# An encoder layer with a Strassen-like MLP: thirteen subtractions move from VectorE to GpSimd, and one weight split is issued later

## The chip, the cores and the metric

The kernel runs as one program on one core of a Trainium2 chip. The metric is the device time of one execution in microseconds (us). TensorE (PE) does the matmuls; a separate row, PEld, shows its weight loads. VectorE (DVE), ScalarE (ACT) and GpSimd (POOL) work on tiles, and SyncE (SP) as well as ACT issue DMA transfers. Every engine works through its own list of instructions in order.

## The reference, cut to what matters

```python
hn = rmsnorm(h, norm_mix); proj = hn @ w_in           # 1024 tokens, 1024 -> 2304
o_a = window_gqa_sink(...); o_b = neighbourhood_attention(...)
h = h + concat(rmsnorm(o_a), rmsnorm(o_b)) @ w_out
hn = rmsnorm(h, norm_ffn)
g, u = hn @ w_gate, hn @ w_up                         # 1024 -> 2816 each
g = depthwise_conv_width3(g) + conv_b
h = h + (silu(g) * u) @ w_down                        # 2816 -> 1024
return rmsnorm(h, norm_final)
```

All data are float32. The kernel keeps that precision on TensorE by splitting each factor into a rounded high part and the rest (the low part) and adding three products: high x high, low x high, high x low.

## The kernel before, in words

**Attention stage, to about 370 us.** The combined projection is cut into 18 tiles of 128 columns (class `Project`, L554). Each tile has weights for eight blocks of the input; they come in two loads of four blocks (`fetch_w`, L152), and each load is split by one ACT instruction that rounds it to the high part and one DVE instruction that subtracts (`halve_w`, L158; the records are L162 and L163). `load` splits the first half, `load_rest` (L562) the second. The generator `rest` (L744) runs through the jobs 3 to 17 and then the output projection, and hands its matmuls out as filler between the attention's own; inside job i, at its block number `REST` = 11 (L757), it calls `load_rest` of job i + 1. Job index 14 is tile 17, the last projected one; its `load_rest` holds its two instructions behind an attention split (`behind`, the second argument of `halve_w`). The order on PE is as written; on the other engines a scheduler sets the order when the program is built.

**MLP stage, from about 400 us.** gate and up are computed for 22 column tiles f, each with seven half-size products instead of eight (a Strassen-Winograd scheme on 2 x 2 halves of input and weights). The input's halves are kept in eight tiles `h1[k]`, `at(k, h)` being half h (512 columns) of tile k. From the normed input come four sums in place, each for k = 0 to 3 (`K1`): the first (`t1`, L1181) and second (`t2`, L1191) of `at(k, 1)`, then in one loop (L1197 to L1199) the third (`t3`, into `at(k, 0)`) and the fourth (`t4`, into `at(k, 1)`). Each sum is split by `operand` (L963): an ACT rounding (L966) and a DVE subtraction (L967), into tiles named `hg`.

A column tile is a `Gated` object (L1090). Its products are PE groups of twelve matmuls: p1 and p2 into the PSUM bank `x`, p5 and then p3 into `y`, p6, then p7 and p4 into `z`. The later group of a bank adds to what is there, and DVE reads the bank between the two (c<-y at L1110 between p5 and p3, gs<-z at L1117 between p6 and p7, c<-z at L1134 between p7 and p4). So p3 can't start on PE before L1110 is done. `conv` (L1123) is two ACT and two DVE instructions of twice the size. p4 ends with a product on DVE (L1140) and, for the first of a pair of column tiles, with a subtraction on the finished block (L1144); `keep` (L1153) sends blocks to DRAM by DMAs from ACT's queue. `sums` (L1159) makes three more subtractions for each pair of column tiles (L1163, L1164, L1167). All these subtractions go through the helper `sub` (L998), so all have the line L998 in the trace.

The first four column tiles, `units` (L1170), are computed together product by product: p5 of all four, p6, p3, p7, p4. Their weights are made by `head_weights` (L1002): loads into three buffers `raw`, a sum or difference on DVE, and the split (`split_w`, L943; ACT L948, DVE L949). After them a loop (L1290 on) takes one column tile at a time in the order p1, p5, p4 of the one before, p6, p2, p3, p7, with `w_next` making the next weights. `owed` (L1289) holds units 1 and 3, whose `sums` come in the first two turns.

GpSimd works in the attention stage: it scales the probabilities (L411), copies sinks (L402) and makes eight bias tiles (L481, L482). Later it has six multiplications at the very end (L1384). Between them it is idle.

Of the kernel before, what the change touches and what calls it, by code (L numbers as in the profile page):

```python
# [16 lines left out]
ALU = mybir.AluOpType  # L17
PSUM = bass.MemoryType.PSUM

D, S, HD = 1024, 1024, 64  # L20
KT = D // 128
NB = S // 128
HALF = 512
# [16 lines left out]
REST = 11  # L40
# [13 lines left out]
def hybrid_layer(tc, xT, w_first, w_in, w_out, w_gate, w_up, w_down, small, sink, rpb, consts, rope, out):  # L54
    nc = tc.nc
    with ExitStack() as ctx:
# [13 lines left out]
        def big(name, tag, dt=F32):  # L70
            return lpool.tile([128, S], dt, name=name, tag=tag, bufs=slots[tag])
# [25 lines left out]
        for name, dst, n in (("h", his, 2), ("h", his, 2), ("l", los, 2), ("l", los, 2), ("w", None, 2)):  # L97
            t = flat(big(name, "mix", F32R)[:, :], n)
# [46 lines left out]
        def behind(*names):  # L145

            stack = ExitStack()
            for n in names:
                stack.enter_context(tc.issue_after(mark[n].ins))
            return stack  # L150
# [7 lines left out]
        def halve_w(raw, held=False):  # L158

            hi, lo = (wpool.tile([128, 4, 128], F32R, name=n, tag=n) for n in ("whi", "wlo"))  # L160
            with behind(*["high", "rest"] * held):
                mark["weights"] = nc.scalar.activation(hi, raw, AF.Copy)  # L162
                mark["weights low"] = nc.vector.tensor_tensor(lo, raw, f32(hi[:, :, :]), op=ALU.subtract)  # L163
            return [(hi[:, j, :], lo[:, j, :]) for j in range(4)]
# [389 lines left out]
        class Project:  # L554
# [5 lines left out]
                self.w = halve_w(raw)  # L560

            def load_rest(self):  # L562
                self.w += halve_w(self.raw, self.m == 17)

            def run(self):
                self.t = tmp("t")
# [50 lines left out]
        xg, first = [None] * KT, [Project(m) for m in range(3)]  # L617
        third = first[2]
        jobs = [Project(m) for m in range(3, 18)] + [OutA(d) for d in range(KT)]

        def split_x(k, part=slice(0, S)):

            g, src = col(C_NMIX + k), xts[k][:, part]
            hi, lo = (t[:, part] for t in xg[k])
            pin(nc.scalar.activation(hi, src, AF.Copy, scale=g))
            pin(nc.vector.scalar_tensor_tensor(lo, src, g, f32(hi), op0=ALU.mult, op1=ALU.subtract))  # L626
# [48 lines left out]
        t = quarters(big("f", "mix"))  # L675
# [5 lines left out]
        for part in range(3):  # L681
            for p, ps in zip(first, banks):
                w, x = p.w[0], xg[0]
# [38 lines left out]
        def make_stacks(job):  # L722
            with tc.high_priority(offset=400):
                stacks(job.m, job.t)
            done.add(job.m)

        def settle(age):

            for item in list(later):
                item[0] -= 1  # L730
                if item[0] <= 0:
                    later.remove(item)
                    item[1]()
            while waiting and (len(waiting) > 1 or age >= (LATE if waiting[0].m == 3 else SOON if waiting[0].m == 17 else LAG)):
                m = waiting[0].m
                if live["op"] + needs(m) > slots["op"]:
                    break
                live["op"] += needs(m)
                with behind(*["stack", "low"] * (m == 3)):
                    waiting.pop(0).post()  # L740
# [3 lines left out]
        def rest():  # L744
            for i, job in enumerate(jobs):
                if i + 1 < len(jobs):
                    with behind(*[["spread", "root"], ["stack"]][i] if i < 2 else []):
                        jobs[i + 1].load()
                for n, _ in enumerate(job.run()):
                    yield True  # L750
                    if i == 0:
                        if n == 8:
                            with behind("copied"):
                                for p in first[:2]:
                                    make_stacks(p)
                        continue
                    if n == REST and i + 1 < len(jobs):  # L757
                        jobs[i + 1].load_rest()
                    settle(n)
                    if (i, n) in aux:  # L760
                        aux[i, n]()
                if i == 0:
                    with behind("stack", "copied"):
                        jobs[1].load_rest()
                    with behind("weights", "weights low"):
                        make_stacks(third)
                if isinstance(job, Project):
                    waiting.append(job)
                while len(waiting) > 2:
                    settle(0)  # L770
                    if len(waiting) > 2:
                        yield False
# [29 lines left out]
        for i in range(8):  # L802
            aux[13, 1 + i + i // 2] = normed_a(*divmod(i, 2))
        filler = rest()
        live["op"] = sum(needs(m) for m in range(3))

# [5 lines left out]
        units = []  # L812
        for g in range(2):
            for b in range(NB):
                q, t = unit_window(g, b)
# [53 lines left out]
        for u in range(len(flat)):  # L869
            q, t, need, kind = flat[u]  # L870
# [51 lines left out]
        for h in range(2):  # L922
            wide = widen(vb2[h], "pt")
            for i in range(4):
                x = mix[4 + i][:, tsl(h)]
# [31 lines left out]
        def group(ps, ws, xs, first, last):  # L957
            for i, (w, x) in enumerate(zip(ws, xs, strict=True)):
                nc.tensor.matmul(ps, w[0], x[0], start=first and i == 0, stop=False, skip_group_check=True)  # L959
                nc.tensor.matmul(ps, w[0], x[1], start=False, stop=False, skip_group_check=True)  # L960
                nc.tensor.matmul(ps, w[1], x[0], start=False, stop=last and i == len(ws) - 1, skip_group_check=True)  # L961
# [12 lines left out]
        at = lambda k, h: h1[k][:, tsl(h)]  # L974
# [20 lines left out]
        HEAD = 4  # L995
        FH = FT // 2
        FO = [f for k in range(FH) for f in (k, k + FH)]
        sub = lambda o, x, y: nc.vector.tensor_tensor(o, x, y, op=ALU.subtract)  # L998

        wsum = [fpool.tile([128, 4, 128], F32, name="ws", tag="tt", bufs=6) for _ in range(HEAD)]  # L1000

# [88 lines left out]
        class Gated:  # L1090
# [45 lines left out]
            def p4(self):  # L1136
                group(self.z, W[self.f, "22"], B["t4"], False, True)
                u = self.c
                nc.vector.tensor_tensor(u[:, 0:HALF], self.z, u[:, 0:HALF], op=ALU.add)
                nc.vector.tensor_tensor(u, u, self.cv, op=ALU.mult)  # L1140
                k = self.f % FH
                if self.f < FH:
                    first_of[k] = u
                    sub(u[:, HALF:S], u[:, HALF:S], u[:, 0:HALF])  # L1144
                    keep(u, ("11", k), ("t1", k))
                else:
                    keep(u, ("21", k), ("22", k))
# [5 lines left out]
        def keep(t, *names):  # L1153
            d = dram.tile([128, HALF * len(names)], F32, name="x", tag="x" + "_".join(f"{n}{k}" for n, k in names))
            nc.scalar.dma_start(d, t)
            for i, name in enumerate(names):
                X[name] = d[:, i * HALF:(i + 1) * HALF]

        def sums(unit):  # L1159
            k = unit.f % FH  # L1160
            a, b = first_of.pop(k), unit.c
            t = big("t23", "mix")
            sub(t[:, 0:HALF], b[:, HALF:S], a[:, HALF:S])  # L1163
            sub(t[:, HALF:S], t[:, 0:HALF], a[:, 0:HALF])  # L1164
            keep(t, ("t2", k), ("t3", k))
            t4 = half("t4")
            sub(t4, b[:, 0:HALF], t[:, 0:HALF])  # L1167
            keep(t4, ("t4", k))

        units = [Gated(f, ("o", "o", "pj", "pj")[i], ("s", "s", "pt", "pt")[i]) for i, f in enumerate(FO[:HEAD])]  # L1170
# [24 lines left out]
            head_weights(i, "s2")  # L1195
        B[2, 2] = [operand(at(k, 1), "op") for k in K2]
        for k in K1:  # L1197
            sub(at(k, 0), at(k, 1), at(k, 0))
            sub(at(k, 1), at(k + 4, 0), at(k, 1))  # L1199
        for i, u in enumerate(units):  # L1200
            u.p6()
            head_weights(i, "s4")
# [87 lines left out]
        for i, f in enumerate(FO[HEAD:]):  # L1290
            u = Gated(f)
# [8 lines left out]
            if pend:  # L1300
                pend.p4()
                if pend.f >= FH:
                    sums(pend)
# [4 lines left out]
            if owed:  # L1308
                sums(owed.pop(0))
# [24 lines left out]
            pend = u  # L1334
        pend.p4()
        sums(pend)


# [76 lines left out]
        for i, (p, j, c) in enumerate(order):  # L1415
# [4 lines left out]
            f, n = PARTS[c]  # L1420
# [146 lines left out]
```

## Time and profile before

| what | value |
|---|---|
| median of 3 runs | 1075.73 us (1075.58 to 1076.07) |
| the profiled execution's own time | 1076.77 us |
| its span, first to last instruction | 1075.0 us |
| granted TensorE clock | 0.997 |
| PE busy | 1063.8 us, 99% of the span, 5094 matmuls |
| DVE busy | 867.3 us, 81% |
| ACT busy | 555.7 us, 52% |
| POOL busy | 106.8 us, 10% |

What lies around the span is 1.77 us. Times inside the trace are microseconds from the start of the span. A row of the timeline has the start, the duration, the engine, the line, the operation, its output and input tiles with shapes, a count, and in brackets the time for which the engine stood idle before it and what ended that. Instructions of one engine overlap a little: the next one's start is often 0.1 us before the recorded end of the one before, so the distance between two starts, not the duration, is what an instruction takes of a full queue.

### The profile page before, as it was taken

The numbers are of one execution on the slowest core, as the hardware profiler recorded it, in microseconds if no ns is written. First come the engines' busy times: TensorE is split into PE (matmuls) and PEld (weight loads), VectorE is DVE, ScalarE is ACT, GpSimd is POOL, SyncE is SP. The second block draws the span as 40 slices with busy tenths as digits, with TensorE's granted clock in tenths as the row PEclk, the third lists the DMA queues.
The fourth block names the chain that finished last, engine by engine and source line by source line (L and its number), as shares of the span: only waits on it lengthen the run. The fifth ranks groups of instructions, "written<-read, shape, count | busy, mean of one in ns | idle before, by whom it ended". The sixth has DMA issues, their size and how long they took to land.

```text
span 1075.0 us, 14902 instructions
## 1 busy us (share of the span) xinstructions
PE 1063.8 (99%) x5094; PEld 889.6 (83%) x5094; DVE 867.3 (81%) x1596; ACT 555.7 (52%) x1059; POOL 106.8 (10%) x188
## 2 busy tenths in 40 slices
PE   9999999999999999999999999999999999999997
PEld 7888888888888888887788888888888888888887
DVE  7889887768878799899988877887887858897765
ACT  8457776647676554534434343432434645544451
POOL 1124333222332000000000000000000000000002
PEclk9999999999999999999999999999999999999998
DMA  7223122322234245214342232322222788867644
GB/s 278 74 74 80 40 69 60 89 69 79 78 88 148 96 156 210 78 56 162 135 157 98 106 110 81 129 106 108 98 89 101 251 288 308 270 216 241 222 139 157
DMA packets 68220, 144.94 MB, mean 135 GB/s; under 512 B 8240, under 2 KB 18736, under 8 KB 68144
## 3 DMA queue, kind: packets, MB, share of 16 engines
q1 hardware_dynamic: 57920, 118.69, 34.9%
q10 hardware_dynamic: 10224, 25.30, 6.2%
q8 instruction: 40, 0.66, 0.2%
q14 instruction: 36, 0.29, 0.1%
HBM read 103.58 MB, written 28.57 MB: 123 GB/s over the span
## 4 chain that ended last, share of the span: by engine, by line
PE 89%; DVE 7%; ACT 1%; issue 1%; DMA 1%; POOL 0%; SPq 0%; DVEq 0%; ACTq 0%
PE pj L170 8%; PE pj L172 8%; PE pj L171 8%; PE dn L959 7%; PE dn L961 7%; PE dn L960 7%; PE z L961 5%; PE z L959 5%; PE z L960 5%; PE s L381 3%; PE x L959 3%; PE x L961 3%; PE x L960 3%; PE y L961 3%; PE y L959 3%; PE y L960 3%
## 5 line engine op out<-in xcount | busy, mean ns | idle before, releaser
L948 ACT ACTIVATE whi<-ws 128x512 fp32r<-128x512 f32 (+1 forms) x100 | 60.3, 623 | 126.8 <-DVE ws L1066 82.5
L959 PE MATMUL dn<-xd,whi 128*128 128x512 f32 (+1 forms) x330 | 124.0, 376 | 0.0
L961 PE MATMUL dn<-xd,wlo 128*128 128x512 f32 (+1 forms) x330 | 123.7, 375 | 0.0
L960 PE MATMUL dn<-xd,whi 128*128 128x512 f32 (+1 forms) x330 | 123.7, 375 | 0.0
L961 PE MATMUL z<-hg,wlo 128*128 128x512 f32 x264 | 103.1, 390 | 0.9 <-DVE wlo L949 0.7
L170 PE MATMUL pj<-xgh,whi 128*128 128x512 f32 x245 | 103.3, 422 | 0.0
L959 PE MATMUL z<-hg,whi 128*128 128x512 f32 x264 | 103.0, 390 | 0.0
L960 PE MATMUL z<-hg,whi 128*128 128x512 f32 x264 | 102.8, 389 | 0.0
L407 ACT ACTIVATE p<-p,nm 128x385 f32<-128x385 f32 (+3 forms) x128 | 75.2, 587 | 50.8 <-DVE nm L403 49.7
L411 POOL TENSOR_SCALAR p<-p,sm 128x384 f32<-128x384 f32 (+1 forms) x128 | 78.1, 622 | 207.2 <-DVE sm L409 171.7
L171 PE MATMUL pj<-xgl,whi 128*128 128x512 f32 x245 | 96.2, 393 | 0.3 <-DVE xgl L626 0.3
L172 PE MATMUL pj<-xgh,wlo 128*128 128x512 f32 x245 | 96.4, 393 | 0.0
L949 DVE TENSOR_TENSOR wlo<-raw,whi 128x512 fp32r<-128x512 f32 (+1 forms) x102 | 66.4, 671 | 26.6 <-ACT whi L948 25.6
L418 DVE TENSOR_TENSOR pl<-pt,ph 128x384 fp32r<-128x384 f32 (+2 forms) x108 | 63.5, 589 | 24.9 <-ACT ph L417 23.5
L948 ACT ACTIVATE whi<-raw 128x512 fp32r<-128x512 f32 (+1 forms) x102 | 60.5, 612 | 44.6 <-DMA raw<-in_w_down_dram 19.8
L949 DVE TENSOR_TENSOR wlo<-ws,whi 128x512 fp32r<-128x512 f32 (+1 forms) x100 | 67.0, 683 | 19.1 <-ACT whi L948 17.9
L1384 POOL TENSOR_TENSOR h<-h,wide 128x256 f32<-128x256 f32 (+1 forms) x6 | 5.4, 918 | 707.4 <-ACT wide L1380 707.4
L417 ACT ACTIVATE ph<-pt 128x384 fp32r<-128x384 f32 (+2 forms) x108 | 55.2, 512 | 32.4 <-PE pt L517 24.7
L961 PEld LDWEIGHTS dn<-xd,wlo 128*128 128x128 f32 x330 | 62.1, 188 | 11.2
L960 PEld LDWEIGHTS dn<-xd,whi 128*128 128x128 f32 x330 | 62.1, 188 | 11.2
L959 PEld LDWEIGHTS dn<-xd,whi 128*128 128x128 f32 x330 | 62.1, 188 | 10.9
L1274 ACT ACTIVATE xd<-xd 128x512 fp32r<-128x512 f32 x77 | 47.6, 626 | 43.8 <-DMA xd<-x 42.1
(270 smaller groups left out, 2678.0 us busy)
## 6 DMA issues: line engine op xcount, KB each, us to landing
xd<-x SPq DMA_DIRECT2D x77, 256.0 KB, 4.8
raw<-in_w_down_dram SPq DMA_DIRECT2D x72, 256.0 KB, 3.8
raw<-in_w_gate_dram SPq DMA_DIRECT2D x22, 512.0 KB, 3.5
raw<-in_w_up_dram SPq DMA_DIRECT2D x22, 512.0 KB, 3.9
x<-c ACTq DMA_DIRECT2D x22, 512.0 KB, 3.3
raw<-in_w_in_dram SPq DMA_DIRECT2D x30, 256.0 KB, 2.8
raw<-in_w_down_dram SPq DMA_DIRECT2D x36, 192.0 KB, 4.2
x<-t ACTq DMA_DIRECT2D x11, 512.0 KB, 2.7
```

What stands on the lines that cost most here:

```text
L170: nc.tensor.matmul(ps, w[0], x[0][:, tsl(h)], start=first, stop=False)
L171: nc.tensor.matmul(ps, w[0], x[1][:, tsl(h)], start=False, stop=False)
L172: nc.tensor.matmul(ps, w[1], x[0][:, tsl(h)], start=False, stop=last)
L407: nc.scalar.activation(p[:, j, 0:e], p[:, j, 0:e], AF.Exp, bias=nm, scale=-1.0, accum_out=sm[:, j:j + 1])
L411: nc.gpsimd.tensor_scalar(p[:, i, 0:m], p[:, i, 0:m], sm[:, i:i + 1], 1.0, op0=ALU.mult, op1=ALU.mult)
L417: mark["high"] = nc.scalar.activation(ph[:, 0:n], ps[:, 0:n], AF.Copy)
L418: mark["rest"] = nc.vector.tensor_tensor(pl[:, 0:n], ps[:, 0:n], f32(ph[:, 0:n]), op=ALU.subtract)
L948: nc.scalar.activation(hi, src, AF.Copy)
L949: nc.vector.tensor_tensor(lo, src, f32(hi[:, :, :]), op=ALU.subtract)
L959: nc.tensor.matmul(ps, w[0], x[0], start=first and i == 0, stop=False, skip_group_check=True)
L960: nc.tensor.matmul(ps, w[0], x[1], start=False, stop=False, skip_group_check=True)
L961: nc.tensor.matmul(ps, w[1], x[0], start=False, stop=last and i == len(ws) - 1, skip_group_check=True)
```

## The change

The helper `sub` gets an argument for the engine. GpSimd then does

- the eight subtractions of the loop over `K1` that make the third and fourth sums;
- the subtraction at the end of p4 for column tiles among the first four (of which two, unit 0 and unit 2, are first of a pair);
- the three subtractions of `sums` for unit 1.

That is 8 + 2 + 3 = 13 subtractions of 128x512. And `load_rest` of the last projected tile is called in its own job, after its third block (n == 2), instead of at block 11 of the job before, and without being held behind the attention's split.

```diff
             def load_rest(self):
-                self.w += halve_w(self.raw, self.m == 17)
+                self.w += halve_w(self.raw)
...
         jobs = [Project(m) for m in range(3, 18)] + [OutA(d) for d in range(KT)]
+        last_in = jobs[14]
...
-                    if n == REST and i + 1 < len(jobs):
+                    if n == REST and i + 1 < len(jobs) and jobs[i + 1] is not last_in:
                         jobs[i + 1].load_rest()
+                    if n == 2 and job is last_in:
+                        job.load_rest()
...
-        sub = lambda o, x, y: nc.vector.tensor_tensor(o, x, y, op=ALU.subtract)
+        sub = lambda o, x, y, engine=nc.vector: engine.tensor_tensor(o, x, y, op=ALU.subtract)
...
                 if self.f < FH:
                     first_of[k] = u
-                    sub(u[:, HALF:S], u[:, HALF:S], u[:, 0:HALF])
+                    sub(u[:, HALF:S], u[:, HALF:S], u[:, 0:HALF], nc.gpsimd if self.f in FO[:HEAD] else nc.vector)
...
             t = big("t23", "mix")
-            sub(t[:, 0:HALF], b[:, HALF:S], a[:, HALF:S])
-            sub(t[:, HALF:S], t[:, 0:HALF], a[:, 0:HALF])
+            engine = nc.gpsimd if unit is units[1] else nc.vector
+            sub(t[:, 0:HALF], b[:, HALF:S], a[:, HALF:S], engine)
+            sub(t[:, HALF:S], t[:, 0:HALF], a[:, 0:HALF], engine)
             keep(t, ("t2", k), ("t3", k))
             t4 = half("t4")
-            sub(t4, b[:, 0:HALF], t[:, 0:HALF])
+            sub(t4, b[:, 0:HALF], t[:, 0:HALF], engine)
...
         for k in K1:
-            sub(at(k, 0), at(k, 1), at(k, 0))
-            sub(at(k, 1), at(k + 4, 0), at(k, 1))
+            sub(at(k, 0), at(k, 1), at(k, 0), nc.gpsimd)
+            sub(at(k, 1), at(k + 4, 0), at(k, 1), nc.gpsimd)
```

## The prediction

> **What bounds the kernel now.** I read the page's busy table first, then the busy time by stretches, then who PE waited for, and last the timeline around each wait.
>
> ```profile
> PE 1063.8 (99%) x5094; PEld 889.6 (83%) x5094; DVE 867.3 (81%) x1596; ACT 555.7 (52%) x1059; POOL 106.8 (10%) x188
> ...
> 460.00:490.00 30.00, 29.89 (x132) 24.48 (x131) 30.00 (x47) 13.46 (x19) 0.00 (x0) 1.00 0.21 70
> 490.00:520.00 30.00, 29.08 (x124) 22.57 (x124) 28.27 (x40) 13.27 (x19) 0.00 (x0) 1.00 0.44 160
> 600.00:700.00 100.00, 100.00 (x442) 82.79 (x442) 80.21 (x113) 41.03 (x61) 0.00 (x0) 1.00 0.30 105
> ```
>
> PE works 99% of the span, so what stops PE anywhere is added at the end, and nothing else counts. The columns of the stretches are length, PE, PEld, DVE, ACT, POOL, clock, DMA share, GB/s. In 600 to 700 PE is full and DVE has a fifth of its time to spare. In 460 to 490 DVE is full (30.00 of 30), in 490 to 520 nearly: there PE hangs on DVE. The PE timeline shows by how little:
>
> ```profile
> 488.99 0.39 PE L960 MATMUL z<-hg,whi 128*128 128x512 f32 x1
> 489.48 0.50 PE L961 MATMUL z<-hg,wlo 128*128 128x512 f32 x1
> ...
> 495.05 0.40 PE L960 MATMUL z<-hg,whi 128*128 128x512 f32 x1
> 495.78 0.50 PE L961 MATMUL z<-hg,wlo 128*128 128x512 f32 x1 [0.34 <-DVE wlo L949]
> ...
> 512.01 0.39 PE L960 MATMUL y<-hg,whi 128*128 128x512 f32 x1
> 512.58 0.50 PE L961 MATMUL y<-hg,wlo 128*128 128x512 f32 x1 [0.18 <-DVE wlo L949]
> ...
> 515.37 0.40 PE L960 MATMUL z<-hg,whi 128*128 128x512 f32 x1
> 516.17 0.50 PE L961 MATMUL z<-hg,wlo 128*128 128x512 f32 x1 [0.40 <-DVE wlo L949]
> ...
> 521.30 0.39 PE L959 MATMUL y<-hg,whi 128*128 128x512 f32 x1
> 521.52 0.39 PE L960 MATMUL y<-hg,whi 128*128 128x512 f32 x1
> ...
> 529.68 0.39 PE L960 MATMUL y<-hg,whi 128*128 128x512 f32 x1
> 530.36 0.49 PE L961 MATMUL y<-hg,wlo 128*128 128x512 f32 x1 [0.29 <-DVE wlo L949]
> ```
>
> Undisturbed, matmuls start 0.22 to 0.23 us apart (521.30 to 521.52). The five steps to a low weight part take 0.49, 0.73, 0.57, 0.80 and 0.68, together 2.1 us too much, and about 2.6 us with slow restarts of some 0.1 us each. That is all that a faster DVE could give back here.
>
> **What is removed.** DVE loses 13 subtractions.
>
> ```profile
> 453.24 0.74 DVE L989 SCALAR_TENSOR_TENSOR h<-h,par,sw 128x512 f32<-128x512 f32 x1
> 453.90 1.28 DVE L998 TENSOR_TENSOR h<-h,h 128x512 f32<-128x512 f32 x2
> ...
> 493.24 0.69 DVE L998 TENSOR_TENSOR ws<-raw 128x512 f32<-128x512 f32 x1 [0.20 <-DMA raw<-in_w_up_dram]
> ...
> 497.44 1.38 DVE L949 TENSOR_TENSOR wlo<-raw,whi 128x512 fp32r<-128x512 f32 x2 [0.51 <-ACT whi L948]
> ...
> 499.78 0.69 DVE L949 TENSOR_TENSOR wlo<-raw,whi 128x512 fp32r<-128x512 f32 x1 [0.36 <-ACT whi L948]
> ...
> 501.11 0.69 DVE L1139 TENSOR_TENSOR c<-z,c 128x512 f32<-128x512 f32 x1 [0.63 <-PE z L961]
> ...
> 517.84 0.68 DVE L1110 TENSOR_TENSOR c<-y,c 128x512 f32<-128x512 f32 x1
> 518.43 1.22 DVE L1140 TENSOR_TENSOR c<-c,cv 128x1024 f32<-128x1024 f32 x1
> ...
> raw<-in_w_gate_dram SPq DMA_DIRECT2D x22, 512.0 KB, 3.5
> ```
>
> An instruction of this size takes 0.60 us of a full queue (517.84 to 518.43). The mark by which I measure is the evacuation at 517.84, c<-y of the fifth column tile: p3 (PE, 521.30 in the fence above) adds to the same bank and can't start before it. Before, DVE is there 3.5 us early.
>
> The order of the built program's instructions shows what now stands ahead of that evacuation. Gone are ten subtractions (eight sums, two finished blocks): -10 x 0.60 = -6.0. New ahead of it are four weight splits and the product of unit 3 that stood behind: 4 x 0.60 + 1.2 = +3.6. DVE's idle time on the way was 0.20 + 0.51 + 0.36 + 0.63 = 1.7; with DVE earlier, the loads, which wait for buffers that DVE frees, show up more. I walked the new order with the old durations and 3.1 to 3.5 us for a weight load (3.5 is the table's median for the larger ones): my estimate is 3.8 us idle, +2.1. So without any other effect the mark starts at 517.84 - 6.0 + 3.6 + 2.1 = 517.5, and all five stalls would go.
>
> **What is added.** GpSimd gets 13 subtractions of 128x512, eight of them from about 454.6 us on, as soon as the first of the second sums (453.90) is there, and five from the first finished block on. Its price for such an operation, and what happens when it meets DVE:
>
> ```profile
> L1384 POOL TENSOR_TENSOR h<-h,wide 128x512 f32<-128x512 f32 x2 | 2.6, 1296 | 691.9 <-ACT wide L1380 691.9
> ...
> L481 POOL TENSOR_TENSOR xb<-cst,rr x8: 983/993/2987, 24.0 to 314.9; 128x384 f32<-128x384 f32 x8
> L482 POOL TENSOR_TENSOR xb<-cst,rr x8: 718/730/1707, 26.9 to 315.9; 128x256 f32<-128x256 f32 x8
> ...
> L163 DVE TENSOR_TENSOR wlo<-raw,whi x38: 670/685/1499, 29.6 to 368.9; 128x512 fp32r<-128x512 f32 x38
> ...
> 248.17 0.99 POOL L481 TENSOR_TENSOR xb<-cst,rr 128x384 f32<-128x384 f32 x1 [1.18 <-DVE nm L403]
> 249.12 1.17 POOL L482 TENSOR_TENSOR xb<-cst,rr 128x256 f32<-128x256 f32 x1
> ...
> 248.22 1.50 DVE L163 TENSOR_TENSOR wlo<-raw,whi 128x512 fp32r<-128x512 f32 x1
> 249.63 1.21 DVE L299 SCALAR_TENSOR_TENSOR kb<-t,cst,ka 128x512 fp32r<-128x512 f32 x1
> ...
> 308.31 1.41 DVE L299 SCALAR_TENSOR_TENSOR kb<-t,cst,ka 128x512 fp32r<-128x512 f32 x2
> ...
> 1050.07 2.55 POOL L1384 TENSOR_TENSOR h<-h,wide 128x512 f32<-128x512 f32 x2 [691.90 <-ACT wide L1380]
> ...
> 1050.02 4.04 DVE L1386 SCALAR_TENSOR_TENSOR h<-h,par,sw 128x512 f32<-128x512 f32 x6 [0.38 <-ACT wide L1380]
> ```
>
> At 248 us four instructions meet that each read two tiles from SBUF. L163 has a median of 0.69 and takes 1.50: it began 0.05 after L481 and lost 0.81. L482 has 0.73 and takes 1.17: it lost 0.44 to L163. L299, 0.70 at 308.31, takes 1.21: it lost 0.51 to L482. So the two engines exclude each other and take turns, though DVE's next instruction was always ready. A turn ends about 0.15 us before the recorded end (248.22 + 0.81 = 249.03 against 249.16). For GpSimd's 1.30 us that is 1.15 us in which DVE stands still. At 1050 DVE reads one tile from PSUM: L1386 runs at 4.04 / 6 = 0.67 beside a busy POOL, L989 at 453.24 to 453.90 takes 0.66 without it. So evacuations from PSUM run beside GpSimd.
>
> [...]
>
> DVE's queue from 454 on is full of weight and operand splits, which read two tiles from SBUF, so every GpSimd subtraction finds it busy. 13 x 1.15 = 14.9; three of them I expect beside an evacuation (0.60 each), -1.8: **+13.1 us** on DVE for 13 x 0.60 = 7.8 taken off. The mark starts at 517.5 + 13.1 = 530.6 and ends its read about 0.55 later: p3 starts at 531.1 instead of 521.30, **+9.8**. This includes all that PE loses on the way (behind the second sums' last block, at the third difference of weights) since DVE's queue alone leads to the mark. Behind it p7 waits for gs<-z two places on, which p3's twelve matmuls (2.7 us) cover. The stall at 529.68 goes, as DVE's remaining work is then no longer behind PE: -0.5.
>
> Also queued behind the new waits: on ACT, the split of the second sums' fourth block stands behind a split that waits for GpSimd's fourth subtraction, and the copy of the fifth tile's p1, which p2 needs, stands behind a DMA issue that waits for a GpSimd block. Both are over before the mark is, so they cost nothing extra. SP's queue is as before but for one pair of transfers swapped. GpSimd's later work (1050) is far off.
>
> **The later split.** It takes one ACT and one DVE instruction out of a crowded place:
>
> ```profile
> 301.51 0.69 DVE L163 TENSOR_TENSOR wlo<-raw,whi 128x512 fp32r<-128x512 f32 x1
> ...
> 304.14 0.38 PE L517 MATMUL pt<-cst,p 128*128 128x128 f32 x2
> 304.59 0.44 PE L528 MATMUL o<-ph,v 128*128 128x384 f32 x1
> 305.18 0.44 PE L529 MATMUL o<-pl,v 128*128 128x384 f32 x1
> ```
>
> From L528 to L529 PE takes 0.59 where a larger matmul takes 0.23, and two transposes and the wait for ph before take 0.45 (304.14 to 304.59). Without the split, the exponentials, and then ph and pl, come up to its 0.60 us earlier: between 0 and -0.6; I take the step's excess, -0.4. The split now stands at its job's third block. Its weights are first used by the ninth: six blocks of three matmuls, at least 6 x 3 x 0.23 = 4.1 us, cover it. Its transfer is issued as before, in `load`. Should the cover fail, it costs at most its own 0.6.
>
> **Sum:** +9.8 - 0.5 - 0.4 = +8.9 us on the profiled 1076.77, whose span is 1075.0 with 1.77 around it (1085.7). The profiled run is 1.04 above the median of the three, so on the median 1075.73 + 8.9 = **1084.6**.
>
> **Rivals.** *No exclusion in this stretch* (the mark 517.5): the stalls go, -2.6 - 0.4, 1072.7. For it speaks that GpSimd was idle there; against it the rows at 248. This one ends on the other side: it decides if a meeting costs DVE under about 0.25 us (p3 has 521.3 - 517.5 - 0.55 = 3.3 us to spare, over 13). *DVE wins when its queue is full* and GpSimd only slips in at evacuations: L481 once took 2.99 us, two more than its median, as if it lost several turns. Then a meeting costs 1.15 - 0.60: 7.2, p3 at 525.2, +3.9 - 0.5 - 0.4 = +3.0, 1078.7. *Losses and gains cancel* within the 0.2% (2.15 us, about what a measurement of this kernel tells from no change): meetings of about 0.3 us, 1075.7. That the change isn't made can't be: the built program has the 13 on POOL.
>
> **Chances.** The forecast (1080 to 1088) 0.60, DVE wins 0.12, cancel 0.11, no exclusion 0.17. So slower 0.72, same 0.11, faster 0.17. The range leaves out the faster case and the tails: 1074.5 to 1088.
>
> **What would show it.** Right: L998 on POOL from 454.6 on with 1.3 to 1.9 us each, DVE's two-SBUF instructions beside it stretched to 1.2 to 1.8, c<-y of the fifth tile near 530, PE stalls of some us at p7 of the third unit and before p3, no change after 600. Wrong: DVE durations of 0.69 beside a busy POOL, or p3 near 519.

## The result and the profile after

The changed kernel takes **1086.07 us** (median of 5 runs, 1085.12 to 1086.80) against 1076.07 (1075.58 to 1076.82) of the kernel before in the same sitting: 10.0 us more, ratio 1.0093 with a 95% interval of 1.0082 to 1.0105. The forecast was 1084.6, 8.9 us more. Run once more with a profile, it took 1086.65 against 1076.31, ratio 1.0093 (1.0076 to 1.0109).

The page of the changed kernel, its busy table:

```profile
PE 1064.9 (98%) x5094; PEld 890.3 (82%) x5094; DVE 867.9 (80%) x1583; ACT 555.6 (51%) x1059; POOL 133.1 (12%) x201
```

DVE has 13 instructions less (1583 for 1596) and is as busy as before (867.9 for 867.3): what it was freed of came back as longer instructions. POOL has 13 more and 26 us more. PE does the same work in a longer span. Whom PE waited for between 440 and 540 us, where before it lost only to low weight parts (columns: us in total, times, longest):

```profile
PE x L962 <- ACT c L1103: 3.1, 1, 3.1
PE z L962 <- ACT whi L951: 2.3, 1, 2.3
PE y L962 <- DVE c L1113: 1.7, 1, 1.7
PE y L964 <- DVE wlo L952: 0.7, 1, 0.7
PE z L964 <- DVE wlo L952: 0.5, 1, 0.5
```

In the head (the work on the first four column tiles) the code's lines have moved by 3 (L1110 is L1113, L998 is L1001). Now the timeline of DVE around the two places where GpSimd works (start, length, then the instruction; in brackets the idle time before it and who ended it):

```profile
457.14 0.69 DVE L1001 TENSOR_TENSOR h<-h,h 128x512 f32<-128x512 f32 x1
457.74 0.68 DVE L1113 TENSOR_TENSOR c<-y,c 128x512 f32<-128x512 f32 x1
458.35 1.18 DVE L952 TENSOR_TENSOR wlo<-ws,whi 128x512 fp32r<-128x512 f32 x1
464.40 1.83 DVE L970 TENSOR_TENSOR hg<-h,hg 128x512 fp32r<-128x512 f32 x1 [4.87 <-ACT hg L969]
...
520.33 0.68 DVE L952 TENSOR_TENSOR wlo<-ws,whi 128x512 fp32r<-128x512 f32 x1
520.93 2.28 DVE L1132 SCALAR_TENSOR_TENSOR cv<-gs,par,cv 128x1023 f32<-128x1023 f32 x1
523.14 1.76 DVE L952 TENSOR_TENSOR wlo<-ws,whi 128x512 fp32r<-128x512 f32 x1
524.82 1.77 DVE L952 TENSOR_TENSOR wlo<-raw,whi 128x512 fp32r<-128x512 f32 x1
526.51 0.68 DVE L1142 TENSOR_TENSOR c<-z,c 128x512 f32<-128x512 f32 x1
527.11 1.17 DVE L952 TENSOR_TENSOR wlo<-raw,whi 128x512 fp32r<-128x512 f32 x1
...
529.34 0.68 DVE L1113 TENSOR_TENSOR c<-y,c 128x512 f32<-128x512 f32 x1
```

Three things are to be seen. The subtractions that make low parts of weights and operands took 0.69 and take 1.17 to 1.83 beside GpSimd (but for the one at 520.33, of which more below). The evacuations c<-y and c<-z, which read PSUM, keep their 0.68. And between 459.53 and 464.40 DVE does nothing: it waits for ScalarE. The mark of the prediction, c<-y of the fifth column tile, starts at 529.34 instead of 517.84. ScalarE at the same time:

```profile
459.01 0.63 ACT L969 ACTIVATE hg<-h 128x512 fp32r<-128x512 f32 x1 [2.82 <-POOL h L1001]
...
463.21 1.15 ACT L969 ACTIVATE hg<-h 128x512 fp32r<-128x512 f32 x2 [1.87 <-POOL h L1001]
```

The second of the two at 463.21 is the one that DVE waits for: the rounding of the last block of the *second* sums, whose input DVE itself had finished at 457.83. It stood 5.9 us in ScalarE's queue behind roundings of the third and fourth sums, which wait for GpSimd. GpSimd's own rows:

```profile
454.37 7.57 POOL L1001 TENSOR_TENSOR h<-h 128x512 f32<-128x512 f32 x3 [96.56 <-DVE h L1001]
461.89 3.78 POOL L1001 TENSOR_TENSOR h<-h,h 128x512 f32<-128x512 f32 x3
...
519.35 2.79 POOL L1001 TENSOR_TENSOR c<-c 128x512 f32<-128x512 f32 x1 [6.48 <-DVE c L1143]
522.10 2.25 POOL L1001 TENSOR_TENSOR t<-c 128x512 f32<-128x512 f32 x1
```

Where DVE is idle, or comes after it, GpSimd takes 3.78 / 3 = 1.26 each. Where both work it takes 1.6 to 2.8, and the first three 7.57, of which the first alone 4.6 (below).

### The profile page after: what moved, and what is told of

Read it like the earlier page. It is cut to its first block, busy times and chain, and to the rows that moved or that the text cites. A ratio compares the mean times of both kernels' runs of the same rounds, so it can differ in the third digit from the quotient of the medians.

```text
span 1084.3 us, 14924 instructions
## 1 busy us (share of the span) xinstructions
PE 1064.9 (98%) x5094; PEld 890.3 (82%) x5094; DVE 867.9 (80%) x1583; ACT 555.6 (51%) x1059; POOL 133.1 (12%) x201
## 4 chain that ended last, share of the span: by engine, by line
PE 89%; DVE 6%; DMA 2%; ACT 1%; issue 1%; POOL 0%; DVEq 0%; SPq 0%; ACTq 0%; POOLq 0%
PE pj L170 8%; PE pj L172 8%; PE pj L171 8%; PE dn L963 6%; PE dn L964 6%; PE dn L962 6%; PE z L962 4%; PE z L964 4%; PE z L963 4%; PE y L962 4%; PE y L964 4%; PE y L963 4%; PE x L962 4%; PE x L964 4%; PE x L963 4%; PE s L381 3%
## 5 line engine op out<-in xcount | busy, mean ns | idle before, releaser
L952 DVE TENSOR_TENSOR wlo<-ws,whi 128x512 fp32r<-128x512 f32 (+1 forms) x100 | 70.1, 712 | 19.1 <-ACT whi L951 17.9
L962 PE MATMUL x<-hg,whi 128*128 128x512 f32 x176 | 69.4, 394 | 3.1 <-ACT c L1103 3.1
L1279 DVE TENSOR_TENSOR xd<-xd 128x512 fp32r<-128x512 f32 x77 | 52.4, 688 | 24.3 <-ACT xd L1278 24.1
```

The lines of the kernel that those rows point to most:

```text
L952: nc.vector.tensor_tensor(lo, src, f32(hi[:, :, :]), op=ALU.subtract)
```

## The experiments

Two theories were put against each other. **A**, the prediction's: GpSimd and DVE exclude each other at SBUF, and each GpSimd subtraction holds DVE for its own length less a little. **B**: the holds are small beside what comes from *later results*, queues that stand behind an instruction that waits for GpSimd.

| kernel | time, us | before, same sitting | ratio (95%) |
|---|---|---|---|
| split_only | 1076.64 | 1076.54 | 1.0001 (0.9992 to 1.0010) |
| sums_only | 1083.28 | 1076.54 | 1.0064 (1.0051 to 1.0077) |
| blocks_only | 1082.28 | 1076.54 | 1.0051 (1.0037 to 1.0065) |
| sums_in_order | 1081.20 | 1076.24 | 1.0046 (1.0032 to 1.0060) |
| after_in_order | 1083.82 | 1076.24 | 1.0070 (1.0058 to 1.0083) |
| eight_idle | 1083.65 | 1076.24 | 1.0070 (1.0057 to 1.0083) |
| fourth_only | 1078.42 | 1076.37 | 1.0021 (1.0012 to 1.0031) |

### The three parts alone

**split_only**: only the edits to `load_rest`, `last_in` and the job loop.

> The kernel before with the later weight split alone. The prediction's step: 0.4 us less, as the stall of PE at 304 us goes and nothing is late for it (ratio 0.9996). Rival, read from the changed kernel's trace, where the stall at 304 us is gone and PE waits 0.8 us near 316 us for the transfer kb<-ka instead: between no change and 0.6 us more (ratio 1.0000 to 1.0006).

No change that can be measured, so the expected gain is not there. The stall at 304 us is gone (the step from L528 to L529 is 0.26 instead of 0.59), and a wait stands 12 us further on that the kernel before doesn't have:

```profile
PE s L381 <- DMA kb<-ka: 0.8, 1, 0.8
```

What feeds that transfer is kb, which DVE makes in two halves (L299). Before, they stand back to back (308.31, x2, in the prediction). DVE's timeline here:

```profile
307.04 0.69 DVE L163 TENSOR_TENSOR wlo<-raw,whi 128x512 fp32r<-128x512 f32 x1
307.65 0.75 DVE L299 SCALAR_TENSOR_TENSOR kb<-t,cst,ka 128x512 fp32r<-128x512 f32 x1
308.39 0.56 DVE L403 CUSTOM_DVE_ANT_0 p<-s,xb 128x384 f32<-128x384 f32 x1
...
308.88 0.68 DVE L545 TENSOR_TENSOR mixb<-o,ot 64x512 f32<-64x512 f32 x1
309.48 0.73 DVE L299 SCALAR_TENSOR_TENSOR kb<-t,cst,ka 128x512 fp32r<-128x512 f32 x1
```

The moved subtraction of the weight split (307.04) now stands ahead of the first half, and a score step (L403) and a sum (L545) between the two. So the second half starts 5.5 us after PE's L529 (303.97), where it was 3.8 (305.18 to 308.97) before and in each of the five other kernels without the later split. The last transfer behind it is issued 9.4 us after that L529 (at 313.33), where it was 8.1 before (313.29), PE waits for it, and the kernel isn't faster.

**sums_only**: in the loop over `K1` both lines get `nc.gpsimd`, as in the change.

> The kernel before with the eight subtractions of the normed input's sums on GpSimd, and nothing else of the change. Theory A, the prediction's (the two engines take turns at SBUF, and every GpSimd subtraction holds VectorE for 1.15 us): eight holds of 1.15 less three of 0.60, less 0.5 of a stall, p3 of the fifth column tile about 5 us later, so 1081 us. Theory B, from the changed kernel's trace (VectorE waits 5.3 us for the results themselves, its holds sum to 3.2 us, and PE is 3.7 us late by 499 us and 2.0 by 518): 2 to 3 us more, 1078 to 1079 us.

6.7 us more, above both expectations. DVE's waits are those of the changed kernel:

```profile
DVE hg L967 <- ACT hg L966: 5.3, 2, 4.9
```

**blocks_only**: the subtraction at the end of p4 and the three of `sums` on GpSimd.

> The kernel before with the five subtractions of finished gated blocks on GpSimd, and nothing else of the change. Theory A: five holds of 1.15 us, of which the slack of 2.8 us before p3 takes half, so about 2 us more, 1078 us. Theory B, from the changed kernel's trace (the store of a finished block waits for GpSimd at the head of ScalarE's queue, and the copy c<-x that frees the next product's bank stands behind it): PE loses 3.1 us there, 1.5 us at the lower clock after it and up to 1.7 us at p3, so 4 to 6 us more, 1080 to 1082 us.

5.7 us more: the size that B named, by A's way. No copy c<-x was late. The timeline of DVE shows four holds in a row:

```profile
513.37 2.32 DVE L1128 SCALAR_TENSOR_TENSOR cv<-gs,par,cv 128x1023 f32<-128x1023 f32 x1
515.61 1.76 DVE L1070 TENSOR_TENSOR ws<-ws,raw 128x512 f32<-128x512 f32 x1
517.29 2.29 DVE L1129 SCALAR_TENSOR_TENSOR cv<-gs,par,cv 128x1023 f32<-128x1023 f32 x1
519.51 1.75 DVE L949 TENSOR_TENSOR wlo<-ws,whi 128x512 fp32r<-128x512 f32 x1
```

L1128 and L1129 take 1.27 alone (506.32 to 507.59 in the same kernel) and L1070 and L949 0.68: each of the four lost 1.01 to 1.08 us. L1070 is the difference of weights from which the next two roundings come, so PE waited 2.0 us for the high part and 2.5 for the low one, and ran at the lower clock for about 5 us after it. Together the parts cost 0.1 + 6.7 + 5.7 = 12.5, more than the whole change with its 10.0. They don't add up, and PE doesn't lose its time in the same place: with the eight alone p3 starts 0.75 us behind c<-y of the fifth column tile (526.72 and 527.47), much as in the changed kernel; with the five alone it starts 3.5 us behind it (525.32 and 528.83), as in the kernel before, so that there the waits for weights set the time and not the mark.

### The price of a meeting by itself

**meetings**: no layer; stretches of subtractions, each begun on both engines by one copy of ScalarE. In the core of it `two` reads two SBUF tiles, `evac` one from PSUM and one from SBUF, `one` is a tensor_scalar:

```python
stretch(two * 24, two * 8)      # VectorE's row, GpSimd's row
stretch(evac * 24, two * 8)
stretch((two * 2 + evac) * 8, two * 8)
stretch(two * 24, one * 8)
stretch(one * 24, two * 8)
```

> No layer at all: VectorE and GpSimd alone in stretches of 128x512 subtractions, begun together by one copy of ScalarE, and the output is a constant. First each engine by itself, then 24 VectorE instructions beside 8 of GpSimd, in five mixes. Theory A (turns, 1.15 us lost by VectorE for each of GpSimd's): 24 at 0.60 and 8 holds of 1.15, some 23.6 us for VectorE's row when both read two SBUF tiles, and 14.4 us when VectorE reads PSUM. Rival (a waiting VectorE goes first, as between 454 and 458 us of the changed kernel, where a GpSimd subtraction took 4.6 us beside five of VectorE at 0.69): VectorE's row stays 14.4 us, and GpSimd's first instruction ends only after it. Third (a turn for GpSimd only where VectorE's queue has a gap or an evacuation from PSUM): as the rival in the plain mix, and about one hold for every evacuation where two subtractions and one evacuation alternate.

The timeline, first each engine alone, then the first two and the last two of these rows:

```profile
4.00 4.29 DVE L71 TENSOR_TENSOR d<-a,b 128x512 f32<-128x512 f32 x7
...
15.89 8.58 POOL L71 TENSOR_TENSOR p<-a,b 128x512 f32<-128x512 f32 x7
...
38.19 22.45 DVE L71 TENSOR_TENSOR d<-a,b 128x512 f32<-128x512 f32 x23
39.35 11.71 POOL L71 TENSOR_TENSOR p<-a,b 128x512 f32<-128x512 f32 x7
...
62.74 13.84 DVE L71 TENSOR_TENSOR d<-bank,a 128x512 f32<-128x512 f32 x23
63.48 8.60 POOL L71 TENSOR_TENSOR p<-a,b 128x512 f32<-128x512 f32 x7
...
100.83 17.23 DVE L71 TENSOR_TENSOR d<-a,b 128x512 f32<-128x512 f32 x23
...
119.89 16.32 DVE L82 TENSOR_SCALAR d<-a 128x512 f32<-128x512 f32 x23
...
131.10 5.11 DVE L82 TENSOR_SCALAR d<-a 128x512 f32<-128x512 f32 x15
```

Alone an instruction of DVE's queue takes 0.60 (seven 4.29, with the end of the last), and 23 that read PSUM take 13.84 beside a busy GpSimd, so nothing is lost there. With two SBUF sources on both sides the 23 take 22.45: (22.45 - 13.84) / 8 = **1.08 us for each GpSimd subtraction**, in strict turns, and GpSimd's own grow from 8.58 / 7 = 1.23 to 11.71 / 7 = 1.67. That is theory A with 1.08 for 1.15. In the mixed row, two subtractions to one evacuation, it is 0.8 (VectorE's 24 take 20.65 us, from 78.07 to 98.72, where 24 with PSUM take 14.4). The Trainium skill's rule ("SBUF — State Buffer", section "Who interferes with whom": a VectorE instruction with two SBUF inputs contends with a GpSimd instruction that reads SBUF, the first to issue holds the shared port for the whole instruction, and a VectorE instruction with at most one SBUF input doesn't contend unless it runs in a mode that uses two ports) agrees in kind; the hold measured is shorter than the 1.23 of the instruction. Two rows I hadn't thought of: a GpSimd with one source costs DVE (17.23 - 13.84) / 8 = 0.42, and a DVE tensor_scalar with *one* source, 0.34 alone (5.11 / 15, its last fifteen, behind GpSimd's end), is held as long as the others, (16.32 - 23 x 0.34) / 8 = 1.06. No run here shows in which mode that tensor_scalar worked.

**eight_idle**: the kernel before, with its order on every engine kept, and after the second sums

```python
for _ in range(8):
    nc.gpsimd.tensor_tensor(idle, f32(B["t2"][0][0]), f32(B["t2"][0][1]), op=ALU.subtract)
```

> The kernel before, every engine's instructions and order unchanged, and eight GpSimd subtractions of 128x512 added from 456 us on: both sources in SBUF, the result (in bfloat16) read by nobody. Theory A: each holds VectorE for 1.07 to 1.15 us in a stretch where VectorE is full, some 9 us, of which the slack of 2.8 us before p3 takes a part: 5 to 7 us more, 1081 to 1084 us. Theory B (the holds cost little, and only results that come later cost): 0 to 1 us more, 1076.5 to 1077.5 us.

7.4 us more, for work whose result nobody reads: B is wrong where it calls the holds small. DVE's row at the end of it, and what PE then waited for:

```profile
468.19 4.58 DVE L967 TENSOR_TENSOR hg<-h,hg 128x512 fp32r<-128x512 f32 x3
```

```profile
PE y L959 <- ACT whi L948: 3.8, 1, 3.8
```

Three subtractions for low parts take 4.58 instead of 1.90, and the weights that are prepared behind them come 3.8 us late. So holds alone, with no result to wait for, cost 7.4 us. That isn't their share in the change: here nothing is taken off DVE, and the change takes 8 x 0.60 = 4.8 off it for these eight. The way isn't the prediction's either: p3 starts 3.5 us behind c<-y (526.15 and 529.62), as before, so PE lost its time earlier, to the late weights and to the matmuls at the lower clock behind that wait, and the slack before p3 hid nothing.

### What the waiting costs on top

**sums_in_order** and **after_in_order**: `operand` gets an argument with which ScalarE's roundings of the second, third and fourth sums keep the order of the program.

```diff
-        def operand(src, tag):
+        def operand(src, tag, pin=lambda i: i):
...
-            nc.scalar.activation(t[:, 0:HALF], src, AF.Copy)
+            pin(nc.scalar.activation(t[:, 0:HALF], src, AF.Copy))
...
-            B["t2"].append(operand(at(k, 1), "xg"))
+            B["t2"].append(operand(at(k, 1), "xg", pin))
```

and so for `t3` and `t4`.

> The kernel with the eight subtractions alone on GpSimd (1083.28 us against 1076.54), and ScalarE's roundings of the second, third and fourth sums kept in the order of the program, so that the last rounding of the second sums no longer stands behind roundings that wait for GpSimd. Theory A (only the holds at SBUF count): nothing changes, 1083 us. Theory B (VectorE's 5.3 us of waiting for that rounding is most of the loss): that wait is gone from VectorE's waits, more of its subtractions meet GpSimd's instead (eight holds of 1.07 less eight times 0.60 saved is 3.8 us, of which the slack of 2.8 us before p3 takes most), and the time is 1077 to 1079 us.

> The changed kernel with the same order of roundings on ScalarE. Theory A: 1086 us as before the edit. Theory B: the 4 to 6 us go that the waiting cost, and what the five finished blocks cost stays: 1081 to 1082 us.

In both the wait in DVE's list is down from 5.3 to

```profile
DVE hg L967 <- ACT hg L966: 0.4, 1, 0.4
```

and the times fall from a ratio of 1.0064 to 1.0046 and from 1.0093 to 1.0070: 1.9 and 2.5 us. The intervals of both pairs overlap, those of the second by 0.0001 alone, and there every run of the one kernel is faster than every run of the other (1084.39 us and less against 1085.12 and more); for the first pair the gain isn't certain. B holds for that much, and not for the 4 to 6 us that I expected of it: with the wait gone DVE works when GpSimd does, and all eight meetings hold it (6.9 us in the trace, where it was 3.2).

**fourth_only**: of the eight only those of the fourth sums on GpSimd.

> The kernel before with four subtractions alone on GpSimd, those of the fourth sums, whose product is the last of the head. Theory A by its plain sum: four holds of 1.07 less four times 0.60 saved, 1.9 us of VectorE, of which the slack before p3 hides a part: 0 to 2 us more, 1076 to 1078 us. Rival (what counts is how the queues are filled around a result that comes late; the eight cost 6.7 us, with that mended 5.0, against 1.9 to 3.8 by the plain sum): half of these, 2.5 to 3.5 us more, 1078.7 to 1079.7 us.

2.0 us more (1.0012 to 1.0031); the plain sum is 4 x (1.08 - 0.60) = 1.9. So even the four whose results are needed last cost more on GpSimd than they free. That the sum fits so well is in part luck: in the trace the four hold DVE for 3.8 us less 2.4 freed, but DVE also waits 1.7 us more than before, and p3 starts 1.3 us behind c<-y, so the slack hid a part of that. For the eight in order the plain sum is 7.4 - 8 x 0.60 = 2.6, and 5.0 was measured; PE's waits there (2.1 us for a weight rounding, 1.8 for c<-x) are behind ScalarE, whose order also changed, and no run separates the remaining 2.4 us.

### What belongs to the change, and what to one execution

**after_again**: the changed kernel unedited.

> The changed kernel once more, for what in its profile belongs to the change and what to one execution. The waits of PE between 440 and 540 us (3.1 us for c<-x, 2.3 for a weight rounding, 1.7 for c<-y), the 4.6 us of GpSimd's first subtraction and the 0.8 us near 316 us for kb<-ka come back if they belong to it. The wait of 1.0 us for VectorE near 1048 us, 2 us after a weight load that came late, is not of the change if it is gone; then the time is nearer 1085 than 1086 us.

The waits are there again, shared out differently, 3.2 us for c<-y and 2.3 for c<-x, and GpSimd's rows lie within 0.4 us of those above. The wait near 1048 us is gone, so it is not of the change. PE in the changed kernel, then in this second execution, and the stretches ahead of p3 and behind its start (PE's busy time is the second figure, the granted clock the third from the right):

```profile
523.76 0.50 PE L962 MATMUL x<-hg,whi 128*128 128x512 f32 x1 [3.14 <-ACT c L1103]
...
530.07 0.50 PE L962 MATMUL y<-hg,whi 128*128 128x512 f32 x1 [1.70 <-DVE c L1113]
...
524.00:528.00 4.00, 4.00 (x12) 2.98 (x11) 4.00 (x4) 1.69 (x3) 3.65 (x3) 0.58 0.15 47
530.00:536.00 6.00, 5.93 (x26) 4.94 (x27) 5.23 (x9) 2.93 (x4) 0.00 (x0) 1.00 0.57 221
```

```profile
523.83 0.50 PE L962 MATMUL x<-hg,whi 128*128 128x512 f32 x1 [2.32 <-ACT c L1103]
...
529.40 0.68 DVE L1113 TENSOR_TENSOR c<-y,c 128x512 f32<-128x512 f32 x1
...
530.13 0.80 PE L962 MATMUL y<-hg,whi 128*128 128x512 f32 x1 [3.25 <-DVE c L1113]
...
524.00:528.00 4.00, 2.88 (x12) 2.00 (x12) 4.00 (x4) 1.76 (x3) 3.72 (x3) 1.00 0.18 57
530.00:536.00 6.00, 5.87 (x14) 4.62 (x15) 2.82 (x6) 1.11 (x2) 0.00 (x0) 0.51 0.57 221
```

In both, p3 starts 0.73 us after the mark, at 530.07 and 530.13, whatever c<-x and the clock did ahead of it. So in the changed kernel it is the mark that p3 waits for. In the first execution PE's clock fell to half ahead of the mark, where PE had to wait anyway, and was full behind it (26 matmuls in 6 us). In the second it fell behind the mark (14 in 6 us), and twelve matmuls at some 0.2 us more are 2.4 us lost for good. The Trainium skill ("TensorE: Matmul & The Clock Gate", "Part 1: The HAM clock gate (the "warmup" mystery)") says that the clock follows PE's activity in a free-running window of some 3.4 us, so that the point at which it changes varies from run to run. These two executions agree: the first has one stretch at a clock of 0.50 between 440 and 540 us, from 524.7 to 528.0 us, about one such window; the second has one twice as long (529.1 to 535.9) and another from 495.0 to 498.3, where the first has none.

### A GpSimd that gets no turn

In every kernel with subtractions of the sums on GpSimd, and in eight_idle, the first of them, which starts while DVE runs back to back, got no turn until DVE read PSUM. In the changed kernel it lasted from 454.37 to 458.98, 4.6 us, and could go on only beside the evacuation at 457.74 in the fence on DVE. The tenth was passed over once, too: it is there from 519.35 on, and still DVE's next instruction, at 520.33, with two SBUF sources, kept its 0.68; only the one behind it was held. In the second execution both are the same (4.61 and 2.79 us). Three kernels without a layer looked for the reason.

**meetings_2**: rows of other kinds, GpSimd begun from inside the row.

> No layer at all, the output is a constant: rows of VectorE's subtractions back to back, and four of GpSimd's that begin when the first or second of the row has ended, as the first of the eight does in the changed kernel, where it took 4.6 us beside five of VectorE at 0.69. The rows differ in one thing each: results written in place, roundings of low parts, the mix of the layer, the shifted sums of the convolution. Theory A (strict turns): GpSimd's first takes at most 1.26 and one VectorE instruction, 1.9 us, in every row. Rival (a GpSimd that starts inside a full row gets no turn until VectorE reads PSUM): 3 us and more in every row without an early evacuation. Third (only some kinds of row keep it out): the kind is seen.

Rows with results in tiles of their own, and the shifted sums, gave GpSimd the next turn (1.64 and 2.17 us). The other rows told nothing: they wrote again to the tile that GpSimd waited for, so it began only late in the row.

**meetings_3**: 26 rows with the start of GpSimd moved in steps.

> No layer at all, the output is a constant: 26 rows of twelve VectorE subtractions back to back, each with three GpSimd subtractions whose first begins a little later than in the row before (steps of 0.04 us through more than 0.5 us, about one period of VectorE), 13 rows with results in tiles of their own, 13 in place. If a GpSimd that starts inside a full row always gets the next turn, its first instruction takes 1.3 to 1.9 us in every row. If the moment of its start decides (0.23 us after a start of VectorE it took 4.6 us in the changed kernel, 0.16 us after one it took 1.64 us in a plain row), some of the rows have a first of over 2.5 us and the others none.

Every first instruction took 1.26 to 1.65 us, none over 2.5. One row of the 26 began before DVE's did and counts for nothing.

**meetings_4**: rows of the layer's own kinds, each result in a tile of its own.

> No layer at all, the output is a constant: 13 rows of ten VectorE instructions back to back, of the kinds that stood beside GpSimd's first subtraction of the eight (which waited 1.6 to 3.3 us for VectorE's next read of PSUM in five kernels, though in all rows of the earlier stretches the first waited for one VectorE instruction only). GpSimd begins when the first or the third of the row has ended; three rows have ScalarE copying beside them. If the kind of instruction keeps GpSimd out (result in place, in the other half of a source's tile, or rounded), the first takes over 2.5 us in the rows of that kind and 1.6 in the others; if ScalarE's work beside it does, in the last three rows alone; if neither, 1.6 us in every row, and the cause stays open.

In all 13 rows 1.57 to 1.63 us, such as

```profile
36.64 1.58 POOL L75 TENSOR_TENSOR p<-h,b 128x512 f32<-128x512 f32 x1 [4.74 <-DVE h L75]
```

So neither the kind of instruction, nor the moment of the start, nor ScalarE's copies beside it is the reason by itself. What kept GpSimd out for 3.3 us in the layer, and let DVE pass it at 520.33, stays open.

## Why the prediction was right, and where its steps were not

The time is 1.5 us from the forecast, and the forecast case is the one that came. The account to the mark, with DVE's busy time from 453.50 to the mark, first before, then after (columns: stretch, length, PE, PEld, DVE, ACT, POOL):

```profile
453.50:517.84 64.34, 63.31 (x274) 50.65 (x273) 62.61 (x94) 29.23 (x42) 0.00 (x0) 1.00 0.27 96
```

```profile
453.50:529.34 75.84, 68.29 (x287) 54.06 (x285) 67.02 (x89) 31.26 (x46) 24.57 (x13) 0.98 0.28 101
```

| step | predicted, us | measured, us |
|---|---|---|
| removed ahead of the mark, and newly ahead of it | -6.0 + 3.6 | 94 to 89 instructions on DVE, as counted |
| holds, whole length beyond the usual | 13 x 1.15 = 14.9, less 1.8 | 7.1, in 9 instructions |
| idle time of DVE | +2.1 | (75.84 - 67.02) - (64.34 - 62.61) = +7.1 |
| the mark | 530.6 | 529.34 |
| p3 starts | 531.1 | 530.07 |

- **PE is bound by DVE in the head, through the mark**: right for the changed kernel, where p3 follows the mark by 0.73 us (I took 0.55) in both executions. It isn't right of every kernel with such holds: in eight_idle and blocks_only PE lost its time to late weights ahead of p3.
- **The price of a meeting**: right in kind, 1.08 where I took 1.15 from the meeting at 248 us. eight_idle shows that holds alone delay this kernel. In the changed kernel they are one of two causes: DVE's holds and its added idle time come to 7.1 us each.
- **"Every GpSimd subtraction finds it busy"**: failed. Three of the first eight ran while DVE waited (between 460.6 and 464.4 us), others met an evacuation, and 9 DVE instructions were stretched by 7.1 us in all (the sum of what each took beyond 0.68, or 1.27 for the shifted sums).
- **"Both are over before the mark is, so they cost nothing extra"**: failed for the split of the fourth block. I saw it stand behind GpSimd in ScalarE's queue and set it at nothing, as it would be over in time. It was; but it held DVE, on whose queue the mark depends, for 4.87 us. Freed of that wait, the kernel was 2.5 us faster (after_in_order). For the copy c<-x the step held: p3 didn't start later for it.
- These two errors have opposite signs, 14.9 - 1.8 - 7.1 = 6.0 too much and 7.1 - 2.1 = 5.0 too little. That the mark came within 1.3 us is owed to it, so the good number is in part luck. It isn't chance alone: while DVE waits it can't be held, so one stands in for the other, and with the wait removed the holds came back.
- **The loads show up by +2.1**: right. Without the 4.87 for the fourth block DVE's idle time is 8.82 - 4.87 = 3.95 us, where I put 3.8. It waited 0.8 for a load itself and 2.9 for three roundings of ScalarE, each of which had waited for a load (for 1.63, 0.99 and 2.07 us), the last of them:

```profile
505.00 1.15 ACT L951 ACTIVATE whi<-raw 128x512 fp32r<-128x512 f32 x2 [2.07 <-DMA raw<-in_w_gate_dram]
505.67 0.69 DVE L952 TENSOR_TENSOR wlo<-raw,whi 128x512 fp32r<-128x512 f32 x1 [2.01 <-ACT whi L951]
```

- **The stall at 529.68 goes**: right.
- **The later split, -0.4**: failed. split_only gives 1.0001. The stall went, and 12 us later PE waited 0.8 us for kb<-ka. I had looked at what the split itself needs in its new place, and not at what comes later on DVE with it there: the second half of kb.
- **No change after 600**: right. The 1.0 us near 1048 didn't come again.
- **Not in the sum**: the half clock behind a stall of PE. p3 came 1.0 us earlier than forecast (8.8 instead of 9.8 later than before) and the time all the same 1.1 later. From p3 to the end of the span it is 553.7 us before, 554.2 in the first execution, with its wait of 1.0 near 1048, and 555.4 in the second, with its 2.4 at half clock.
- Of the rivals, *DVE wins when its queue is full* described the first of the 13 and, for one instruction, the tenth; *no exclusion* is refuted by eight_idle and meetings.

No version here beats the kernel before. By the plain sum a subtraction of 128x512 costs DVE 1.08 on GpSimd and 0.60 on DVE, where DVE's queue is full of instructions with two SBUF sources.

## What to carry to other kernels

In these runs, subtractions moved from VectorE to GpSimd relieved VectorE only as far as it read PSUM or was idle meanwhile; against instructions with two SBUF sources a GpSimd subtraction held it longer (1.08 us) than it would have taken itself (0.60). When a result moves to a slower engine, look along every in-order queue for instructions that stand behind one that waits for it, and ask not only if they are done in time but whom they keep from working until then. The same holds for an instruction moved to a quieter place: what stands behind it there may be on the path.

## What the runs showed of the hardware

- The exclusion isn't a matter of two sources alone: VectorE's tensor_scalar with one SBUF source of 128x512 in f32, 0.34 us alone, lost 1.06 us to each GpSimd subtraction. A GpSimd tensor_scalar with one source cost VectorE's two-source subtractions 0.42 us.
- GpSimd loses too: 1.67 us a turn instead of 1.23.
- A wait of PE of 1.8 to 3.8 us was mostly followed by 3 to 12 matmuls in a row at 0.43 us instead of 0.23; in the changed kernel the wait of 2.3 us that ends at 494.76 wasn't, and in the second execution the same wait, of 2.2 us, was.
